# Hybrid attention block on one core: weight differences on VectorE, projections placed between block products, gate products moved behind the scores

## The chip, the core and the metric

The kernel runs on one core of a Trainium2 chip. TensorE (PE, with its weight loads shown as PEld) multiplies matrices into PSUM; VectorE (DVE), ScalarE (ACT) and GpSimd (POOL) do elementwise work; SyncE (SP) issues most of the loads. The metric is the time of one execution on the device in microseconds.

## The reference

One transformer block on 512 tokens of width 1024, in float32. The input is normalised (rmsnorm) and multiplied by one wide matrix `w_in`, whose columns are split into the parts of two branches:

```python
n = rmsnorm(h, g_mix[l])
proj = n @ w_in[l]
(gq, gk, gv, gr, z_gf, z_gb, cq, ckv, kr, z_ma, z_mb) = jnp.split(proj, SPLIT_IDX, axis=-1)
...
merged = jax.nn.sigmoid(z_ma) * y_gla + jax.nn.sigmoid(z_mb) * y_mla
h = h + merged @ w_out[l]
m = rmsnorm(h, g_mlp[l])
h = h + jnp.square(jax.nn.relu(m @ w_ff1[l])) @ w_ff2[l]
```

The first branch is a gated linear attention (GLA) with 4 heads, forward and backward over the tokens. Its decays come from a small gate product, `log_sigmoid(z @ w_gate + b) / 16`, summed along the tokens; query and key are multiplied by exponentials of these sums before their product is formed. Its output is normalised per head and multiplied by `silu(gr)`. The second branch is a latent attention with 8 heads, rotary positions and a softmax (MLA). Each branch is weighted by a sigmoid gate (`z_ma`, `z_mb`). An output product and a squared-ReLU feed-forward part with a residual each follow, and a last rmsnorm.

## The kernel before, in words

**Precision and tiles.** Every float32 operand of a matrix product is split into a rounded high half and a low half (`split`, L92 to L98): ScalarE writes the high half (L93, or L97 with a scale), VectorE subtracts it to get the low half (L94, L98). A product is then three matmuls, high by high, high by low, low by high (`mm3`, L87 to L90). Tiles are 128 partitions by 512 tokens or columns, tile `u2`, or two of these side by side, tile `u4`; both kinds come from pools with a fixed number of buffers (29 and 26). Split weights lie in pools `wh` and `wl` with 4 buffers each, unsplit ones in `wf` with 3. PSUM has two pools, `mm` and `at`, of four banks each.

**Stage 1, first products (up to about 28 us).** The first rows of weights, for gq0, gk0 and two of the MLA gates (zb0, zb1), are multiplied while the input arrives, and the norm of the input is formed.

**Stage 2, three block products (about 28 to 200 us).** The 1024 wide projections gr, za and gv are each formed by `Seven`: both operands are cut into 2 by 2 blocks and seven block products are made in place of eight, in the order `SEVEN = (1, 2, 5, 6, 3, 7, 4)`. The sums and differences of the input blocks are made once (`x_sums`, `more_x_sums`, tiles xy, xz, split to xsy, xsz). The weights come as four blocks of two tiles each (`load`), and four of the seven products use a difference of blocks, made in place by `less` (L571 to L575) on POOL, two instructions of 128x1024 each, so 24 instructions in all. `prepare(m)` makes the difference if one is needed and splits the block; `product(m)` runs the 24 matmuls, for each of two row blocks rb and each of four input tiles p, and then copies or adds the accumulators (L615, L620) and hands finished rows to a sink: `gr_rows` (L628, L629), `za_rows` (L633, L635) or `gv_rows` (L97, L98). Accumulators xs and zs each serve several of the seven products one after the other. The loop (L907 to L926) prepares two steps ahead. The projection zb3 (`zb_gate(3)`) stands behind product 7 of gr, gq1 (`project_qk(1, 0)`) behind product 7 of gv. `gate_parts(0, "mm")` stands behind product 3 of gv.

**Stage 3, four GLA heads (about 200 to 360 us).** For each head h the loop (L931 to L981) emits: `gla_scores` (product bd and its copy bds on ACT, L497; four tiles sc with matmuls L505, L506, L507; a masked overwrite from bds, L511; a split); `gla_turn` of the head before (transposes, tile y, L678); `project_qk(h + 1, 1)` (gk of the next head); `gate_parts(h + 1)`; `gla_out` (48 matmuls, squares L660 and gating L662, then the norm factor on POOL, L663 to L665, and four scalings of the output rows on POOL, L668); for the first two heads `zb_gate(4 + h)` and `project_qk(h + 2, 0)`; `gla_qk` of the next head. `gate_parts` is a chain: gate product L410, Abs, Exp, Ln on ACT (L411, L415, L416), a scan on VectorE (L425), small copies on POOL (L436 to L438), Exp on ACT (L433, L434, L440). `gla_qk` then multiplies query and key by these on VectorE (L454), and POOL makes from them the factors for neighbouring and far chunks (L462, eight instructions per head). For head 2, `rotary_tables` stands ahead of the scores: the positions are loaded by a DMA that POOL issues (L730), VectorE forms the angle (L732 to L743), ACT sine and cosine (L744, L745). For the last head the latent projections ckv and cq come ahead of the scores; `latent` is a generator that yields halfway through its first projection.

**Stages 4 to 6.** MLA attention, the output product and the feed-forward part, from about 360 us to the end.

**What sets the order.** The instructions of an engine run in order. The framework places them, but helpers pin the order of some: `in_program_order(ordered, PE_ONLY)` at L927 pins TensorE to the written order through stage 2, the next line pins POOL from `x_sums` to there, and `goes_behind` (L124) puts a group behind another. In stage 3 TensorE's order is pinned only in these places. Loads stand on SP's queue and wait there for a free buffer.

Of the kernel before, what the change touches and what calls it, by code (L numbers as in the profile page):

```python
# [14 lines left out]
AF = mybir.ActivationFunctionType  # L15
# [3 lines left out]
P = 128  # L19
# [37 lines left out]
def tile_block(ctx: ExitStack, tc: tile.TileContext, t, out: bass.AP):  # L57
# [49 lines left out]
    def traced():  # L107
        return len(nc.cur_bb.bb.instructions)
# [447 lines left out]
    class Seven:  # L556
# [13 lines left out]

        def less(self, dst, x, y):  # L571
            for g in range(2):
                nc.gpsimd.tensor_tensor(  # L573
                    self.blocks[dst][g], self.blocks[x][g], self.blocks[y][g], op=ALU.subtract
                )  # L575

# [17 lines left out]
        def product(self, m):  # L594
            if m == 1:
                self.xs = [ps("at", f"{self.name}x{rb}") for rb in range(2)]
                self.c11, self.c12, self.c22 = ([u2(f"{self.name}{c}") for _ in range(2)] for c in "abc")
            elif m == 2:
                self.ws = [ps("mm", f"{self.name}w{rb}") for rb in range(2)]
            elif m == 5:  # L600
                self.zs = [ps("at", f"{self.name}z{rb}") for rb in range(2)]
            accs = {2: "ws", 5: "zs", 3: "zs"}.get(m, "xs")
            accs = getattr(self, accs)
            begin = m in (1, 2, 5)
            right = self.right.pop(m)
            for rb in range(2):
                acc, tok = accs[rb], slice(rb * P, (rb + 1) * P)
                for p in range(KD // 2):
                    lh, ll = x_left[p][m]
                    wh, wl = right[p // 2]  # L610
                    mm3(acc, lh[:, tok], ll[:, tok], wh[:, p % 2, :], wl[:, p % 2, :],
                        begin and p == 0, p == KD // 2 - 1, not begin)
                if m in (1, 5, 6):
                    c = {1: self.c11, 5: self.c22, 6: self.c12}[m][rb]
                    nc.scalar.activation(c, acc, AF.Copy)  # L615
                elif m == 4:
                    self.sink(2 + rb, 0, acc, u2(f"{self.name}d"))
                else:
                    c = {2: self.c11, 3: self.c12, 7: self.c22}[m][rb]
                    nc.vector.tensor_tensor(c, acc, c, op=ALU.add)  # L620
                    self.sink(rb + (2 if m == 7 else 0), int(m != 2), c, c)
# [23 lines left out]
    def gla_out(h, sc):  # L645

        half, at = h // 2, (h % 2) * GDV
        accs = [ps("at", f"gla{h}o{j}") for j in range(2)]
        c = slice(at, at + GDV)
        for i in range(NT):  # L650
            o = accs[i // 2][:, (i % 2) * GDV : (i % 2 + 1) * GDV]
            tok = slice(i * P, (i + 1) * P)
            for j in range(NT):
                mm3(o, sc[j][:, 0, tok], sc[j][:, 1, tok], v[j, half][:, 0, c], v[j, half][:, 1, c],
                    j == 0, j == NT - 1)
        tot = sm(f"gla{h}ss")
        for i in range(NT):
            o = accs[i // 2][:, (i % 2) * GDV : (i % 2 + 1) * GDV]
            junk = u2(f"gla{h}sq")
            nc.scalar.activation(junk[:, 0:GDV], o, AF.Square, accum_out=tot[:, i : i + 1])  # L660
            g = g1[i, half][:, c]
            nc.vector.tensor_tensor(g, o, g, op=ALU.mult)  # L662
        nc.gpsimd.tensor_scalar(tot, tot, 1.0 / GDV, EPS, op0=ALU.mult, op1=ALU.add)  # L663
        nc.gpsimd.tensor_tensor(tot, tot, mhalf.to_broadcast([P, NT]), op=ALU.pow)
        nc.gpsimd.tensor_tensor(tot, tot, r_x, op=ALU.mult)  # L665
        for i in range(NT):
            g = g1[i, half][:, c]
            nc.gpsimd.tensor_scalar(g, g, tot[:, i : i + 1], None, op0=ALU.mult)  # L668

    def gla_turn(h, early=None):  # L670

# [16 lines left out]
    def latent(col, n, gcol, name):  # L688
        cs, sqs = [], []
        for j in range(n):  # L690
            if j == 0:
                begun = proj_begin(w_in, col, f"{name}0")
                proj_run(begun, xT, None, range(KD // 2))
                yield
                acc = proj_run(begun, xT, None, range(KD // 2, KD))
            else:
                acc = proj_T(col + j * P, f"{name}{j}")
            c = u2(f"{name}c{j}")
            nc.scalar.activation(c, acc, AF.Copy, scale=gvec[:, gcol + j : gcol + j + 1])
            s = u2(f"{name}s{j}")  # L700
            nc.scalar.activation(s, acc, AF.Square)
            if sqs:
                nc.vector.tensor_tensor(s, s, sqs[-1], op=ALU.add)
            cs.append(c)
            sqs.append(s)
        yield
        diag = feature_rstd(sqs[-1], n * P, name, True)
        yield
        rs = spread(diag, name, "mm")
        res = []  # L710
        for j in range(n):
            nc.vector.tensor_tensor(cs[j], cs[j], rs, op=ALU.mult)
            hl = u4(f"{name}hl{j}")
            split(hl[:, 0, :], hl[:, 1, :], cs[j])
            res.append(hl)
        yield res
# [176 lines left out]
    def zb_gate(f):  # L893
        g2.append(gated(proj_T(C_ZB + f * P, f"zb{f}"), f"b{f}")[1])
# [5 lines left out]
    summed = traced()  # L900
    x_sums()
    zb_gate(2)
    steps = [(a, m) for a in range(3) for m in SEVEN]
    ordered = traced()
    for a, m in steps[:2]:
        sevens[a].prepare(m)
    for n, (a, m) in enumerate(steps):  # L907
        if n + 2 < len(steps):
            b, mm = steps[n + 2]
            if a + 1 < 3:  # L910
                for x in {3: (0,), 7: (2, 1), 4: (3,)}.get(m, ()):
                    sevens[a + 1].load(x)
        if m == 7:
            sevens[a].product(m)
            if a == 0:
                zb_gate(3)
            elif a == 2:
                project_qk(1, 0)
        if n + 2 < len(steps):
            sevens[b].prepare(mm)  # L920
            if n == 0:
                more_x_sums()
        if m != 7:
            sevens[a].product(m)
        if a == 2 and m == 3:
            parts = gate_parts(0, "mm")  # L926
    in_program_order(ordered, PE_ONLY)  # L927
    in_program_order(summed, (mybir.EngineType.Pool,))
    near, nxt, far = gla_qk(0, parts)
    scored = None  # L930
    for h in range(GH):  # L931
        last = h == GH - 1
        began = traced()
        if h == GH - 2:
            cos, sin = rotary_tables()
        if last:
            ckv_steps, cq_steps = latent(C_CKV, 2, V_KV, "ckv"), latent(C_CQ, 3, V_Q, "cq")
            next(ckv_steps)
            next(ckv_steps)
            marks = [traced()]  # L940
            next(cq_steps)
            marks.append(traced())
            next(ckv_steps)
            marks.append(traced())
            next(cq_steps)
            goes_behind((marks[1], marks[2]), (marks[0], marks[1]), PE_ONLY)
            goes_behind((marks[2], traced()), (marks[1], marks[2]), PE_ONLY)
            ckv = next(ckv_steps)
            next(cq_steps)
            zb = proj_T(C_ZB + 6 * P, "zb6")  # L950
        projected = traced()
        sc = gla_scores(near, nxt, far)
        scored = traced()
        goes_behind((projected, scored), (began, projected), PE_ONLY)
        if h:
            gla_turn(h - 1, (projected, scored))
        if last:
            g2.append(gated(zb, "b6")[1])
            spreading = traced()
            cq = next(cq_steps)  # L960
            goes_behind((spreading, traced()), (projected, scored), PE_ONLY)
            kbuf = rotary_k()
            zb = proj_begin(w_in, C_ZB + 7 * P, "zb7")
            at = traced()
            proj_run(zb, xT, None, range(3))
            mid = traced()
            ro = rotary_q()
            goes_behind((mid, traced()), (at, mid), PE_ONLY)
            g2.append(gated(proj_run(zb, xT, None, range(3, KD)), "b7")[1])
            for _ in up_units(0):  # L970
                pass
            gla_out(h, sc)
        else:
            project_qk(h + 1, 1)
            parts = gate_parts(h + 1)
            gla_out(h, sc)
            if h < 2:
                zb_gate(4 + h)
            if h < 2:
                project_qk(h + 2, 0)  # L980
            near, nxt, far = gla_qk(h + 1, parts)  # L981
    LAG_B, LAG_C = 3, 6
    units = iter(())
# [367 lines left out]
```

## Time and profile before

| | |
|---|---|
| median of 3 runs | 824.61 us (821.28 to 826.24) |
| the profiled execution | 824.34 us, span 822.6 us |
| granted clock, mean over the span | 0.974 |
| PE / PEld busy | 772.7 / 646.2 us |
| DVE / ACT / POOL busy | 605.0 / 450.7 / 202.6 us |
| POOL on `less` (L573), 24 instructions | 70.6 us |

The span runs from the first to the last instruction of the profiled execution. A row of a group names the line, the engine, the operation and the tiles (output, arrow, inputs), then the total and the mean of one instruction, then the idle time of the engine ahead of it and what ended that. A row of the waits names who waited for whom, the total, how often, and the longest. A row of a stretch gives its length, then busy time and number of instructions of PE, PEld, DVE, ACT and POOL, the granted clock of TensorE, and the DMA share and rate. A row of the timeline gives start, duration and instruction, and in brackets the idle time before it.

### The profile page before, as it was taken

Reading aid. Unit: us, or ns where it says so; the run is one execution under the profiler, and the core shown is the slowest. Engines: PE = TensorE matmul, PEld = TensorE weight load, DVE = VectorE, ACT = ScalarE, POOL = GpSimd, SP = SyncE. Lnnn points to the kernel's source line nnn. Section 1 sums busy time; section 2 is a strip of 40 time slices with the busy share of each in tenths; the row PEclk is TensorE's granted clock in tenths of the full one; section 3 lists DMA queues with packets and bytes.
Section 4 is the critical chain, followed back from the end, with each engine's and each line's share of the span. In section 5 each row is a group of like instructions: output and inputs, shape, how many; then the busy total and the mean of one; then the engine's idle time right before and its main releaser. Section 6 shows DMA issues by size and latency. Waiting matters only on the chain.

```text
span 822.6 us, 10202 instructions
## 1 busy us (share of the span) xinstructions
PE 772.7 (94%) x3744; PEld 646.2 (79%) x3744; DVE 605.0 (74%) x838; ACT 450.7 (55%) x761; POOL 202.6 (25%) x230
## 2 busy tenths in 40 slices
PE   9976999978978889999999999999999999999996
PEld 7755777857867678898888888888888888888885
DVE  7898689997746474779997367795679567956795
ACT  7654455564635373579885246643564356435654
POOL 1884273725437062333112010000000000000014
PEclk9997999998989799999999999999999999999998
DMA  7814313003012103134203363136213611360002
GB/s 251 287 58 131 99 51 103 1 26 104 26 51 78 39 8 51 33 71 135 65 26 129 103 233 101 51 103 197 60 51 103 202 55 51 104 203 26 27 1 102
DMA packets 87042, 73.95 MB, mean 90 GB/s; under 512 B 15088, under 2 KB 66288, under 8 KB 86992
## 3 DMA queue, kind: packets, MB, share of 16 engines
q1 hardware_dynamic: 85904, 70.14, 28.5%
q10 hardware_dynamic: 864, 2.38, 0.8%
q0 software_dynamic: 224, 0.79, 0.3%
q8 instruction: 29, 0.48, 0.2%
q14 instruction: 21, 0.17, 0.1%
HBM read 69.62 MB, written 2.10 MB: 87 GB/s over the span
## 4 chain that ended last, share of the span: by engine, by line
PE 70%; DVE 13%; ACT 6%; POOL 6%; issue 3%; DMA 0%; POOLq 0%; DVEq 0%; ACTq 0%
PE f L89 7%; PE f L90 7%; PE f L88 7%; PE gx L88 4%; PE gx L90 4%; PE gx L89 4%; PE first L312 2%; POOL qk L462 2%; PE wo L89 2%; PE wo L88 2%; PE gz L90 2%; PE gz L89 2%; PE wo L90 2%; PE gz L88 2%; PE tp L870 2%
## 5 line engine op out<-in xcount | busy, mean ns | idle before, releaser
L1290 POOL DMA_DIRECT2D gfin<-in_g_final x1 | 0.7, 661 | 282.7 <-PE f L90 282.7
L1115 DVE TENSOR_TENSOR w<-w,w 128x1024 f32<-128x1024 f32 x32 | 38.7, 1220 | 0.4
L573 POOL TENSOR_TENSOR zaw<-zaw,zaw 128x1024 f32<-128x1024 f32 x8 | 22.2, 2801 | 32.8 <-DVE za10l L94 20.7
L573 POOL TENSOR_TENSOR gvw<-gvw,gvw 128x1024 f32<-128x1024 f32 x8 | 25.0, 3164 | 18.9 <-DVE gv10l L94 14.3
L573 POOL TENSOR_TENSOR grw<-grw,grw 128x1024 f32<-128x1024 f32 x8 | 23.4, 2955 | 3.2 <-DVE gr50l L94 3.0
L888 POOL TENSOR_TENSOR tb<-tb,y 128x512 f32<-128x512 f32 x8 | 11.2, 1402 | 50.3 <-DVE tb L887 36.0
L856 ACT ACTIVATE e<-s,top 128x512 f32<-128x512 f32 x32 | 22.1, 693 | 2.4 <-DVE top L853 2.3
L1062 DVE TENSOR_TENSOR h<-gx,h 128x512 f32<-128x512 f32 x32 | 21.5, 683 | 1.9 <-PE gx L90 1.8
L94 DVE TENSOR_TENSOR pT<-tp,pT 128x512 fp32r<-128x512 f32 x32 | 21.6, 678 | 1.0 <-ACT pT L93 0.7
L853 DVE TENSOR_REDUCE top<-s 128x1 f32<-128x512 f32 x32 | 21.7, 679 | 0.1
L93 ACT ACTIVATE pT<-tp 128x512 fp32r<-128x512 f32 x32 | 19.2, 600 | 3.4 <-PE tp L870 3.4
L870 PE MATMUL tp<-ident,e 128*128 128x128 f32 x128 | 19.3, 273 | 0.1
L88 PE MATMUL av<-pT,v 128*128 128x256 f32 x64 | 19.1, 299 | 0.0
L436 POOL COPY v3f<-rrf 128x4 f32<-128x4 f32 x4 | 0.9, 234 | 72.5 <-DVE rrf L425 72.5
L1168 ACT ACTIVATE fa<-f 128x512 f32<-128x512 f32 x32 | 18.5, 578 | 0.0
L89 PE MATMUL av<-pT,v 128*128 128x256 f32 x64 | 18.4, 287 | 0.0
L90 PE MATMUL av<-pT,v 128*128 128x256 f32 x64 | 18.2, 285 | 0.0
L870 PEld LDWEIGHTS tp<-ident,e 128*128 128x128 f32 x128 | 15.3, 140 | 3.7 <-PE s L90 0.6
L93 ACT ACTIVATE gbh<-y 128x512 fp32r<-128x512 f32 x16 | 10.1, 634 | 14.0 <-DVE y L1185 14.0
L506 PE MATMUL sc<-qk 128*128 128x128 f32 x32 | 8.6, 362 | 9.8 <-POOL qk L462 9.8
L93 ACT ACTIVATE sc<-sc 128x512 fp32r<-128x512 f32 x16 | 9.2, 594 | 15.5 <-DVE sc L511 15.5
L506 PEld LDWEIGHTS sc<-qk 128*128 128x128 f32 x32 | 6.8, 264 | 10.4 <-POOL qk L462 10.4
(1637 smaller groups left out, 2995.3 us busy)
## 6 DMA issues: line engine op xcount, KB each, us to landing
w<-in_w_ff SPq DMA_DIRECT2D x64, 256.0 KB, 3.3
grw<-in_w_in SPq DMA_DIRECT2D x8, 512.0 KB, 9.1
zaw<-in_w_in SPq DMA_DIRECT2D x8, 512.0 KB, 3.9
gvw<-in_w_in SPq DMA_DIRECT2D x8, 512.0 KB, 4.2
x<-in_xt SPq DMA_DIRECT2D x8, 256.0 KB, 5.4
vw<-in_w_first SPq DMA_DIRECT2D x8, 256.0 KB, 5.6
h<-in_x ACTq DMA_DIRECT2D x4, 512.0 KB, 5.2
out<-ms SPq DMA_DIRECT2D x7, 256.0 KB, 2.2
```

Of the source, the lines that this page charges most:

```text
L88: nc.tensor.matmul(acc, lh, rh, start=start, stop=False, skip_group_check=onto)
L89: nc.tensor.matmul(acc, lh, rl, start=False, stop=False, skip_group_check=onto)
L90: nc.tensor.matmul(acc, ll, rh, start=False, stop=stop, skip_group_check=onto)
L93: nc.scalar.activation(hi, src, AF.Copy)
L94: rest.tensor_tensor(lo, src, raw(hi), op=ALU.subtract)
L573: nc.gpsimd.tensor_tensor(self.blocks[dst][g], self.blocks[x][g], self.blocks[y][g], op=ALU.subtract)
L853: nc.vector.tensor_reduce(top, acc, axis=AX.X, op=ALU.max, negate=True)
L856: nc.scalar.activation(e, acc, AF.Exp, bias=top, accum_out=tot)
L870: nc.tensor.transpose(tp[:, k * P : (k + 1) * P], e[:, k * P : (k + 1) * P], ident)
L1062: nc.vector.tensor_tensor(hc, acc, hc, op=ALU.add)
L1115: nc.vector.tensor_tensor(wq[dst][g], wq[x][g], wq[y][g], op=op)
L1168: nc.scalar.activation(a, acc, AF.Relu)
```

## The change

`less` issues its subtractions on VectorE. `product` runs the input tiles in the outer loop and the two row blocks in the inner one, and handles both accumulators after all 24 matmuls. The four scalings at the end of `gla_out` go from POOL to ACT. The projections that stand between block products are listed in a table: zb3 behind product 2 of gr, zb4 behind product 7 of gr, gq1 behind product 7 of za, gk1 behind product 7 of gv, zb5 behind product 4 of gv; in a step with such a projection the product and the projection come ahead of the preparation two steps on. In the heads, `gate_parts(h + 1)` uses pool `mm` and stands directly behind the scores and transposes; for heads 0 and 1 gq of head h + 2 follows, then `gla_out`, then gk of head h + 2; for head 2 the first projection of ckv, whole, and then `gla_out`. `latent` yields behind its first projection rather than halfway. TensorE's written order is now pinned from stage 2 to `gla_out` of head 2. The diff, all of it:

```diff
--- before.py
+++ after.py
@@ -570,7 +570,7 @@
 
         def less(self, dst, x, y):
             for g in range(2):
-                nc.gpsimd.tensor_tensor(
+                nc.vector.tensor_tensor(
                     self.blocks[dst][g], self.blocks[x][g], self.blocks[y][g], op=ALU.subtract
                 )
 
@@ -603,13 +603,14 @@
             accs = getattr(self, accs)
             begin = m in (1, 2, 5)
             right = self.right.pop(m)
-            for rb in range(2):
-                acc, tok = accs[rb], slice(rb * P, (rb + 1) * P)
-                for p in range(KD // 2):
-                    lh, ll = x_left[p][m]
-                    wh, wl = right[p // 2]
-                    mm3(acc, lh[:, tok], ll[:, tok], wh[:, p % 2, :], wl[:, p % 2, :],
+            for p in range(KD // 2):
+                lh, ll = x_left[p][m]
+                wh, wl = right[p // 2]
+                for rb in range(2):
+                    tok = slice(rb * P, (rb + 1) * P)
+                    mm3(accs[rb], lh[:, tok], ll[:, tok], wh[:, p % 2, :], wl[:, p % 2, :],
                         begin and p == 0, p == KD // 2 - 1, not begin)
+            for rb, acc in enumerate(accs):
                 if m in (1, 5, 6):
                     c = {1: self.c11, 5: self.c22, 6: self.c12}[m][rb]
                     nc.scalar.activation(c, acc, AF.Copy)
@@ -665,7 +666,7 @@
         nc.gpsimd.tensor_tensor(tot, tot, r_x, op=ALU.mult)
         for i in range(NT):
             g = g1[i, half][:, c]
-            nc.gpsimd.tensor_scalar(g, g, tot[:, i : i + 1], None, op0=ALU.mult)
+            nc.scalar.activation(g, g, AF.Copy, scale=tot[:, i : i + 1])
 
     def gla_turn(h, early=None):
 
@@ -690,9 +691,8 @@
         for j in range(n):
             if j == 0:
                 begun = proj_begin(w_in, col, f"{name}0")
-                proj_run(begun, xT, None, range(KD // 2))
+                acc = proj_run(begun, xT)
                 yield
-                acc = proj_run(begun, xT, None, range(KD // 2, KD))
             else:
                 acc = proj_T(col + j * P, f"{name}{j}")
             c = u2(f"{name}c{j}")
@@ -900,42 +900,39 @@
     summed = traced()
     x_sums()
     zb_gate(2)
+    fillers = {
+        (0, 2): lambda: zb_gate(3), (0, 7): lambda: zb_gate(4), (1, 7): lambda: project_qk(1, 0),
+        (2, 7): lambda: project_qk(1, 1), (2, 4): lambda: zb_gate(5),
+    }
     steps = [(a, m) for a in range(3) for m in SEVEN]
     ordered = traced()
     for a, m in steps[:2]:
         sevens[a].prepare(m)
     for n, (a, m) in enumerate(steps):
-        if n + 2 < len(steps):
-            b, mm = steps[n + 2]
-            if a + 1 < 3:
-                for x in {3: (0,), 7: (2, 1), 4: (3,)}.get(m, ()):
-                    sevens[a + 1].load(x)
-        if m == 7:
+        ahead = steps[n + 2] if n + 2 < len(steps) else None
+        filled = (a, m) in fillers
+        if a + 1 < 3:
+            for x in {3: (0,), 7: (2, 1), 4: (3,)}.get(m, ()):
+                sevens[a + 1].load(x)
+        if filled:
             sevens[a].product(m)
-            if a == 0:
-                zb_gate(3)
-            elif a == 2:
-                project_qk(1, 0)
-        if n + 2 < len(steps):
-            sevens[b].prepare(mm)
+            fillers[a, m]()
+        if ahead:
+            sevens[ahead[0]].prepare(ahead[1])
             if n == 0:
                 more_x_sums()
-        if m != 7:
+        if not filled:
             sevens[a].product(m)
         if a == 2 and m == 3:
             parts = gate_parts(0, "mm")
-    in_program_order(ordered, PE_ONLY)
     in_program_order(summed, (mybir.EngineType.Pool,))
     near, nxt, far = gla_qk(0, parts)
-    scored = None
     for h in range(GH):
         last = h == GH - 1
-        began = traced()
         if h == GH - 2:
             cos, sin = rotary_tables()
+        began = traced()
         if last:
-            ckv_steps, cq_steps = latent(C_CKV, 2, V_KV, "ckv"), latent(C_CQ, 3, V_Q, "cq")
-            next(ckv_steps)
             next(ckv_steps)
             marks = [traced()]
             next(cq_steps)
@@ -971,13 +968,16 @@
                 pass
             gla_out(h, sc)
         else:
-            project_qk(h + 1, 1)
-            parts = gate_parts(h + 1)
-            gla_out(h, sc)
-            if h < 2:
-                zb_gate(4 + h)
+            parts = gate_parts(h + 1, "mm")
             if h < 2:
                 project_qk(h + 2, 0)
+                gla_out(h, sc)
+                project_qk(h + 2, 1)
+            else:
+                ckv_steps, cq_steps = latent(C_CKV, 2, V_KV, "ckv"), latent(C_CQ, 3, V_Q, "cq")
+                next(ckv_steps)
+                gla_out(h, sc)
+                in_program_order(ordered, PE_ONLY)
             near, nxt, far = gla_qk(h + 1, parts)
     LAG_B, LAG_C = 3, 6
     units = iter(())
```

## The prediction, made before the change was run

> **What bounds the kernel now.** I read the page's busy line and its groups first, then the waits of TensorE, then the busy time by stretches, then the order of instructions around each long wait.
>
> ```profile
> span 822.6 us, 10202 instructions
> PE 772.7 (94%) x3744; PEld 646.2 (79%) x3744; DVE 605.0 (74%) x838; ACT 450.7 (55%) x761; POOL 202.6 (25%) x230
> L1115 DVE TENSOR_TENSOR w<-w,w 128x1024 f32<-128x1024 f32 x32 | 38.7, 1220 | 0.4
> L573 POOL TENSOR_TENSOR zaw<-zaw,zaw 128x1024 f32<-128x1024 f32 x8 | 22.2, 2801 | 32.8 <-DVE za10l L94 20.7
> L573 POOL TENSOR_TENSOR gvw<-gvw,gvw 128x1024 f32<-128x1024 f32 x8 | 25.0, 3164 | 18.9 <-DVE gv10l L94 14.3
> L573 POOL TENSOR_TENSOR grw<-grw,grw 128x1024 f32<-128x1024 f32 x8 | 23.4, 2955 | 3.2 <-DVE gr50l L94 3.0
> ```
>
> TensorE (PE) is busy 94% of the span, so the time can only shrink where it stands still or runs slowly. The change touches the stretch from about 28 to 346 us. TensorE's waits there:
>
> ```profile
> PE sc L506 <- POOL qk L462: 9.8, 3, 4.4
> PE grx L89 <- DVE gr60l L94: 9.8, 1, 9.8
> PE ckvss L255 <- DVE ckvs L703: 3.9, 1, 3.9
> PE sc L505 <- ACT bds L497: 2.8, 1, 2.8
> PE bd L493 <- DVE qkb L454: 1.9, 1, 1.9
> PE zaz L89 <- DVE za30l L94: 1.7, 1, 1.7
> PE gvz L89 <- DVE gv30l L94: 1.7, 1, 1.7
> PE zax L89 <- DVE za61l L94: 1.7, 1, 1.7
> PE gvz L89 <- DVE gv31l L94: 1.7, 1, 1.7
> PE grz L89 <- DVE gr50l L94: 1.6, 1, 1.6
> ```
>
> Two kinds stand here. In the block products (gr, za, gv) it is the low half of a split weight on VectorE (DVE) that is late; in the heads it is the qk factors from GpSimd (POOL). The rows add to 36.6 us; waits below 1 us are left out. The clock adds to that: after the 9.8 us wait a matmul takes 0.63 us that takes 0.39 elsewhere (the gate product below, of the same shape), and the granted clock falls in each of these places.
>
> ```profile
> 68.06 0.80 PE L89 MATMUL grx<-gr60l,xsy 128*128 128x512 f32 x1 [9.79 <-DVE gr60l L94]
> 68.65 0.63 PE L90 MATMUL grx<-gr60h,xsy 128*128 128x512 f32 x1
> 58.00:77.00 19.00, 8.83 (x28) 6.41 (x27) 17.56 (x11) 6.23 (x9) 12.23 (x5) 0.73 0.21 58
> 196.00:209.00 13.00, 9.94 (x44) 8.31 (x43) 7.50 (x13) 2.62 (x5) 6.86 (x8) 0.74 0.29 81
> 229.00:239.00 10.00, 6.12 (x26) 5.45 (x27) 2.90 (x7) 2.42 (x5) 4.40 (x6) 0.66 0.22 62
> 267.00:287.00 20.00, 16.43 (x61) 13.32 (x62) 10.17 (x19) 6.40 (x10) 1.99 (x4) 0.74 0.14 41
> 300.00:320.00 20.00, 16.13 (x68) 13.08 (x68) 11.24 (x18) 8.94 (x19) 13.93 (x16) 0.91 0.27 31
> ```
>
> The columns of a stretch are length, busy time of PE, PEld, DVE, ACT, POOL, then the clock. Length times missing clock is at most 5.1, 3.4, 3.4, 5.2 and 1.8 us; part of that fell on an idle engine, so I count 2.8, 2.8, 2.4, 4.7 and 1.7, together 14.4. What can be won at all is thus near 51 us.
>
> Why the low halves are late: stretches with and without a subtraction on POOL.
>
> ```profile
> 52.60:70.20 17.60, 7.81 (x29) 6.14 (x30) 17.60 (x8) 5.42 (x8) 17.60 (x6) 0.81 0.05 12
> 150.30:169.20 18.90, 16.42 (x70) 12.61 (x68) 17.53 (x9) 8.09 (x10) 18.89 (x7) 1.00 0.00 1
> 70.20:89.60 19.40, 17.71 (x69) 13.35 (x68) 15.53 (x19) 12.96 (x17) 0.03 (x1) 0.91 0.66 206
> L94 DVE TENSOR_TENSOR gr61l<-grw,gr61h 128x1024 fp32r<-128x1024 f32 x1 | 3.4, 3378 | 0.0
> L94 DVE TENSOR_TENSOR gr30l<-grw,gr30h 128x1024 fp32r<-128x1024 f32 x1 | 1.2, 1228 | 0.3 <-ACT gr30h L93 0.3
> L620 DVE TENSOR_TENSOR zaa<-zaw,zaa 128x512 f32<-128x512 f32 x2 | 1.4, 678 | 0.0
> ```
>
> In the first two stretches (12 subtractions and one small POOL instruction) VectorE finishes 17 instructions in 35.1 us, 2.07 us each; in the third 19 in 15.5 us, 0.82 each. The same split takes 3.38 us beside POOL and 1.23 without it. L620, one of whose inputs is a PSUM accumulator, keeps 0.68 us even beside POOL.
>
> **The change part by part.** *Subtractions on VectorE.* 24 instructions leave POOL (22.2 + 25.0 + 23.4 = 70.6 us) and come to VectorE at 1.22 us each by L1115, the same shape: 29.3 us more. What VectorE gets back in the two stretches, which hold half of the 24, is 17 × (2.07 − 0.82) = 21 us; over all 24, by count, up to 42, and no less than 21. So VectorE's load in the stage changes by between +8 and −13 us, and I take −10, since every stretch with back-to-back subtractions looks like these two. A weight is ready after 1.2 + 1.0 + 1.2 us instead of 3 + 1.0 + 3.4.
>
> The Trainium skill, SBUF — State Buffer, section "Who interferes with whom", says that a VectorE instruction with two SBUF inputs and a GpSimd instruction that reads SBUF exclude one another for a whole instruction, and that one with a single SBUF input is not held up. The long gr61l and the short L620 agree. By the rule alone up to the whole 70.6 us could come free, which would end all waits of the block products and give some 4 us less than the sum below, inside the forecast's own range.
>
> *Fillers and the order inside a product.* zb3 moves from behind gr7 to behind gr2, zb4, gk1 and zb5 come into the stage, gq1 goes behind za7. Each costs TensorE 24 matmuls at 16.42/70 = 0.235 us, 5.6 us, wherever it stands: zero in sum, but each covers 5.6 us of VectorE's work. Each also brings a split (1.04 ACT, 1.23 DVE) and an evacuation (0.68) with it. Their weights pass SP's queue earlier, one 512 KB load each; zb4's was issued at 89.7 and first read at 188.8, so its cover is about 99 us. Behind gr7 it has hardly any left if it is issued as late as before; the nearest price is the 3.6 us from issue to use of the positions load below. With p outside rb, a product wants its second half-weight 12 matmuls (2.7 us) in rather than 6, frees the first after 12 rather than 18, and ends both accumulators together, so the first accumulator's evacuation starts 2.7 us later. That matters only where the next product adds to the same bank, 7 then 4; a filler now stands between these in all three blocks.
>
> ```profile
> 89.70 0.37 SPq L222 DMA_DIRECT2D zb4f<-in_w_in  x1
> L93 ACT ACTIVATE zb4h<-zb4f x1: 1042/1042/1042, 188.8 to 188.8; 128x1024 fp32r<-128x1024 f32 x1
> ```
>
> It is issued when zb3's split frees its slot, and that split now comes some 30 us earlier, so I charge nothing. Term a, block gr: waits of 1.6 + 9.8 and 2.8 of clock, 14.2. TensorE reached gr6's second matmul at 68.06 − 9.79 = 58.3; without the 1.6 and with zb3 in front it gets there at 62.3, and at the second half-weight 2.7 later. VectorE ended gr5's splits about where the first stretch begins, 52.6, and from there has the four half-size xsz, less6, gr6, zb3 and gra: 2.7 + 2.4 + 2.5 + 1.2 + 1.4 = 10.2, plus 2.4 for less5: near 65 if all of it comes first, near 62 if gra and zb3 do not. gr3 and gr7 follow as closely. I leave 2 us of waits: **−12.2**. What is late next is the second half-weight of gr6, then gr3. Bounds −7 to −14.2. Term b, za and gv: waits of 4 × 1.7; VectorE has 14 × 1.23 + 8 × 1.22 + 14 × 0.68 = 36.5 us of work per block (splits, subtractions, sums and gates) against 7 × 5.6 = 39 of TensorE, and a filler brings 1.9 against 5.6. I leave 2 us: **−4.8**, bounds −6.8 to +6 (two us on three late weights).
>
> *Gate products behind scores, scaling on ACT.* The chain gate product, Exp, Ln, scan, Exp, qk, POOL's factors decides when a head's scores can go on.
>
> ```profile
> 244.04 0.39 PE L410 MATMUL gatef<-z,gate_f 128*128 128x512 f32 x1
> 262.52 2.80 POOL L668 TENSOR_SCALAR gra<-gra,gla1ss 128x256 f32<-128x256 f32 x2
> 265.30 1.81 POOL L668 TENSOR_SCALAR grd<-grd,gla1ss 128x256 f32<-128x256 f32 x2
> 267.74 0.49 PE L506 MATMUL sc<-qk 128*128 128x128 f32 x2 [4.23 <-POOL qk L462]
> 268.21 0.78 POOL L730 DMA_DIRECT2D pos_i<-in_positions  x1
> 271.80 0.43 DVE L732 CAST ang<-pos_i 128x512 f32<-128x512 int32 x1 [8.18 <-DMA pos_i<-in_positions]
> 278.83 0.57 ACT L497 ACTIVATE bds<-bd 128x512 f32<-128x512 f32 x1
> L660 ACT ACTIVATE gla0sq<-gla0o x4: 366/376/384, 220.1 to 222.8; 128x256 f32<-128x256 f32 x4
> ```
>
> From the gate product of head 2 (244.0) to the end of the factors (268.2, when POOL goes on) it is 24.2 us, 4.6 of it the four scalings that POOL now loses: 19.6. TensorE meanwhile has gq and gk, 2 × 5.6, and gla_out, 48 matmuls of half the width or again 5.6: 17, plus 1 of bd (8 matmuls of a quarter): a wait of 1 to 2 us instead of 4. Four scalings on ACT have no row; the nearest is L660, same shape, 0.37, and above it the 0.68 of L620's 128x512 on VectorE: 1.5 to 2.7 us a head, no gain or loss where ACT is half idle. Term c, head 0: its gates stand where they stood, with four products behind them, but no subtractions slow VectorE; of 1.9, the 9.8 − 4.4 − 4.2 = 1.2 of its factors, and 2.8, **−2.5** (0 to −5.9). Term d, head 1: of 4.4 + 2.4, 1.3 stays: **−5.5** (−2 to −6.8). Term e, head 2: old loss 4.2 + 2.8 + 4.7 = 11.7. POOL finishes some 5 us sooner, but the positions load is queued behind the factors, and from its issue to bds it is 10.6 us, with gk3 no longer there to fill: TensorE's order is now fixed through head 2, sc3 needs bds's bank, and gates, ckv0 and gla_out stand behind it. I leave 1 + 7.5 + 2.7 = 11.2: **−0.5** (+6 to −10). Term f, head 3: cq0 whole instead of half ahead of ckvss, 2.7 more cover, of 3.9 + 1.7, hence **−3** (0 to −5.6). Term g: the last head's scalings fall in a stretch where ACT is full, 1.5 us of which I charge **+0.5** (0 to +2.7).
>
> ```profile
> 360.00:380.00 20.00, 19.87 (x127) 17.34 (x126) 17.60 (x37) 19.35 (x48) 10.30 (x15) 1.00 0.24 69
> ```
>
> The sum is −12.2 − 4.8 − 2.5 − 5.5 − 0.5 − 3 + 0.5 = −28.0. The profiled execution took 824.34 us (span 822.6), 0.3 below the median of 824.61, so the forecast is **796.3 us**.
>
> **The rivals.** *Rotary gets out of the way* (chance 0.17): if the framework puts bds ahead of the sine table on ACT, or issues the positions load before the factors, term e becomes −10: 787. For: bds needs only the bd product, nothing of the sine. Against: in the row above it came last, behind both tables, though bd was multiplied before the factors were ready.
>
> *VectorE paces the stage* (0.18): VectorE is full in the stretch around gr6 (17.60 of 17.60) and now carries 1.2 us of subtraction ahead of each split itself; if every second step of gr and a third of za and gv waits 1 to 1.5 us, and the chain of head 0 stays, terms a to c give −6 instead of −19.5: 810. The Trainium skill, Perfetto Trace Analysis, section "Identifying the Most-Contended Engine", would have the engine with the highest occupancy relieved first; by that rule a move onto a VectorE that is 100% busy from 52.6 to 70.2 is wrong. The trace speaks half against it, since 0.82 of 2.07 us there is work and the rest is being held up.
>
> *Slower: the long splits are not POOL's doing* (0.07). Place: 40 to 180 us. VectorE then carries 29.3 us more on top, of which the slack where POOL is silent (19.4 − 15.5 per stretch, three such) takes 12 at best; the heads save 11: 831 to 843, and 834 because the slack is mostly there. Without it, it decides once less than 29.3 − 11 = 18 us of the 21 to 42 come free. Against it: the pairs 3.38 and 1.23 above.
>
> *The gain is handed back* (0.08): the tiles of head 1 and 2 come early but their buffers do not, since more gates and one more gk are held through the heads; the waits only move: 822.
>
> **How the numbers follow.** The forecast has 0.50, its own range 786 to 806. 787, 796 and 810 hold 0.85 of the chance and are all more than 1% (8 us, about what a measurement of this kernel can tell from no change) below 824.6. Same is the fourth rival, 0.08, slower the third, 0.07. With terms a and c at their good ends beside the first rival, and 810 with a little more, the range is 780 to 814.
>
> **What would show it.** Right: no L94 row above 2 us between 60 and 170 us; L573 on DVE at 1.2; POOL below 125 us busy; the 9.8 us wait gone and gr6 below 2; the three qk waits below 2 each. Wrong: za or gv with new waits above 1 us per product, the rotary wait above 12 us, or ckvss as late as before. It fails as a whole if L94 stays long with POOL silent.

## The result, and the profile after

The changed kernel takes 800.62 us (median of 4 runs, 797.92 to 800.86) against 824.59 before: a ratio of 0.9707, 95% interval 0.967 to 0.9743, 24 us faster. The forecast was 796.3 us with a range of 780 to 814. The profiled execution took 800.71 us, its span is 799.0. First the page's busy line, then the subtractions on VectorE (DVE) from the groups between 40 and 180 us, then TensorE's (PE) waits from 28 to 330 us:

```profile
span 799.0 us, 10180 instructions
...
PE 765.6 (96%) x3744; PEld 643.6 (81%) x3744; DVE 587.1 (73%) x862; ACT 458.4 (57%) x777; POOL 118.0 (15%) x190
```
```profile
L573 DVE TENSOR_TENSOR zaw<-zaw,zaw 128x1024 f32<-128x1024 f32 x8 | 9.8, 1223 | 0.2
L573 DVE TENSOR_TENSOR gvw<-gvw,gvw 128x1024 f32<-128x1024 f32 x8 | 9.8, 1222 | 0.2
L573 DVE TENSOR_TENSOR grw<-grw,grw 128x1024 f32<-128x1024 f32 x6 | 7.3, 1213 | 0.0
```
```profile
PE sc L505 <- ACT bds L497: 10.7, 1, 10.7
PE zb L90 <- DVE zb3l L94: 2.9, 1, 2.9
PE ckvss L255 <- DVE ckvs L703: 2.7, 1, 2.7
PE sc L506 <- POOL qk L462: 2.2, 2, 1.2
PE bd L493 <- DVE qkb L454: 1.6, 1, 1.6
PE y L679 <- DVE sc L94: 1.5, 2, 1.3
...
PE sc L507 <- POOL qk L462: 1.0, 2, 0.8
```

VectorE does 24 instructions more and is busy 18 us less. Every wait of the block products is gone but one, at zb3. In the heads the long waits were for POOL's factors (9.8 us in all before, 3.2 now); now the longest, 10.7 us, is for ScalarE's (ACT) copy bds.

Where the 23.6 us of the span went is read from the starts of the same instruction in both traces. Before:

```profile
100.29 0.39 PE L88 MATMUL zax<-za10h,xT 128*128 128x512 f32 x1
...
174.35 0.39 PE L410 MATMUL gatef<-z,gate_f 128*128 128x512 f32 x1
...
208.75 0.40 PE L410 MATMUL gatef<-z,gate_f 128*128 128x512 f32 x1
...
237.71 0.38 PE L678 MATMUL y<-ident,gra 128*128 128x128 f32 x2
...
286.67 0.40 PE L410 MATMUL gatef<-z,gate_f 128*128 128x512 f32 x1
...
353.32 0.28 PE L88 MATMUL gla3o<-gv,sc 128*128 128x256 f32 x1
```

After:

```profile
91.74 0.39 PE L88 MATMUL zax<-za10h,xT 128*128 128x512 f32 x1
...
162.46 0.39 PE L410 MATMUL gatef<-z,gate_f 128*128 128x512 f32 x1
...
196.21 0.58 PE L410 MATMUL gatef<-z,gate_f 128*128 128x512 f32 x1
...
221.64 0.41 PE L679 MATMUL y<-ident,gra 128*128 128x128 f32 x2 [1.29 <-DVE sc L94]
...
258.04 0.78 PE L410 MATMUL gatef<-z,gate_f 128*128 128x512 f32 x1
...
328.85 0.28 PE L88 MATMUL gla3o<-gv,sc 128*128 128x256 f32 x1
```

A projection that changed its stretch is worth 5.6 us there, as in the prediction; ckv0's 11 matmuls that used to stand ahead of the gates of head 3 are 2.6.

| stretch, term | difference of the marks | work that came or went | change | predicted |
|---|---|---|---|---|
| to the first za product (a) | −8.6 | +5.6 (zb4) | −14.2 | −12.2 |
| to the gates of head 0 (b) | −3.3 | +5.6 (gq1) | −8.9 | −4.8 |
| to the gates of head 1 (c) | −0.7 | 0 | −0.7 | −2.5 |
| to the transposes of head 0 (d) | −3.5 | 0 | −3.5 | −5.5 |
| to the gates of head 3 (e) | −12.6 | −11.2 (zb5, one gk), −2.6 | +1.2 | −0.5 |
| to gla_out of head 3 (f) | +4.2 | +2.6 | +1.6 | −3 |
| to the end (g) | +0.9 | 0 | +0.9 | +0.5 |

The last column adds to −28.0, the one before it to −23.6. Terms a and c vary between traces of the same code by up to 2.8 us each, as shown further down, so their single figures here are rough.

### The profile page after: what moved, and what is told of

Read it like the earlier page. It is cut to its first block, busy times and chain, and to the rows that moved or that the text cites. A ratio compares the mean times of both kernels' runs of the same rounds, so it can differ in the third digit from the quotient of the medians.

```text
span 799.0 us, 10180 instructions
## 1 busy us (share of the span) xinstructions
PE 765.6 (96%) x3744; PEld 643.6 (81%) x3744; DVE 587.1 (73%) x862; ACT 458.4 (57%) x777; POOL 118.0 (15%) x190
## 4 chain that ended last, share of the span: by engine, by line
PE 76%; DVE 7%; ACT 6%; POOL 5%; issue 2%; DMA 2%; SPq 0%; POOLq 0%; DVEq 0%; ACTq 0%
PE f L89 7%; PE f L90 7%; PE f L88 7%; PE gx L88 4%; PE gx L90 4%; PE gx L89 4%; POOL qk L462 3%; PE wo L90 2%; PE wo L88 2%; PE gz L90 2%; PE gz L88 2%; PE gz L89 2%; PE wo L89 2%; PE tp L870 2%; DMA x<-in_xt 1%
## 5 line engine op out<-in xcount | busy, mean ns | idle before, releaser
L870 PEld LDWEIGHTS tp<-ident,e 128*128 128x128 f32 x128 | 15.5, 140 | 3.6 <-PE s L90 0.4
L505 PE MATMUL sc<-qkf 128*128 128x128 f32 x32 | 7.4, 319 | 10.8 <-ACT bds L497 10.7
L888 POOL TENSOR_TENSOR tb<-tb,y 128x512 f32<-128x512 f32 x8 | 11.2, 1404 | 43.9 <-DVE tb L887 30.5
L505 PEld LDWEIGHTS sc<-qkf 128*128 128x128 f32 x32 | 6.7, 226 | 12.5 <-ACT bds L497 11.6
L88 PE MATMUL s<-kbuf,q 96*128 96x512 f32 x32 | 14.0, 438 | 0.7 <-ACT e L856 0.5
L93 ACT ACTIVATE b_10h<-w 128x1024 fp32r<-128x1024 f32 x7 | 7.4, 1059 | 12.1 <-PE gz L90 6.0
L93 ACT ACTIVATE b_20h<-w 128x1024 fp32r<-128x1024 f32 x7 | 7.4, 1059 | 12.1 <-PE gz L90 6.0
```

What stands on the lines that cost most here:

```text
L88: nc.tensor.matmul(acc, lh, rh, start=start, stop=False, skip_group_check=onto)
L93: nc.scalar.activation(hi, src, AF.Copy)
L870: nc.tensor.transpose(tp[:, k * P : (k + 1) * P], e[:, k * P : (k + 1) * P], ident)
```

## The experiments

Each time is the median of the experiment's own runs beside runs of the kernel before on the same chip, with the ratio to these and its 95% interval. The changed kernel stands at 0.9707 by the same measure. Differences between two experiments are taken from these medians; the ratios would give up to 2 us more or less.

**e1, the subtractions alone.** The kernel before with one edit, as in the diff:

```diff
-                nc.gpsimd.tensor_tensor(
+                nc.vector.tensor_tensor(
```

> The kernel before with the 24 weight differences on VectorE and nothing else changed. Theory (VectorE was held up by GpSimd's subtractions): the splits fall back to 1.2 us, the waits of za and gv (6.8 us) go, of the 9.8 us wait and its slow clock about 5 stay because no projection stands ahead of gr5: 15 us less than before, about 809. Rival (the projections between the products and the product order bring the gain, the engine of the subtraction does not matter): within 4 us of before, 820 to 826. Second rival (VectorE has no room for 29 us more): 5 to 15 us slower than before.

803.83 us, 0.9761 (0.9733 to 0.9789): 19.7 us of the 24. VectorE's busy time falls by 14 us although it has 29.3 more to do, and no split is longer than 2 us. The page's busy line and TensorE's waits:

```profile
PE 770.2 (96%) x3744; PEld 646.9 (80%) x3744; DVE 590.6 (73%) x862; ACT 451.3 (56%) x761; POOL 134.1 (17%) x206
```
```profile
PE sc L506 <- POOL qk L462: 9.4, 3, 4.4
...
PE grz L89 <- DVE gr50l L94: 2.0, 1, 2.0
...
PE grx L89 <- DVE gr60l L94: 1.2, 1, 1.2
```

The 9.8 us wait becomes 1.2 with no projection in front of it; za and gv have no wait above 1 us. Both rivals are out. It is 5 us better than my own theory said, which had left 5 us of waiting at gr6.

**e2, all but the subtractions.** The changed kernel with `less` on POOL again:

```diff
-                nc.vector.tensor_tensor(
+                nc.gpsimd.tensor_tensor(
```

> The changed kernel with the 24 weight differences back on GpSimd. Theory: splits beside a subtraction take about 3.4 us again, waits return in gr, za and gv, partly covered by the projections: 10 to 18 us more than the changed kernel, 811 to 819. Rival (projections and order bring the gain): at most 4 us more, 800 to 805.

822.68 us, 0.9999 (0.9986 to 1.0013): nothing at all is left of the gain, 3 to 4 us worse than expected. TensorE's waits:

```profile
PE sc L505 <- ACT bds L497: 10.7, 1, 10.7
PE zb L90 <- DVE zb3l L94: 10.6, 1, 10.6
PE zb L88 <- ACT zb3h L93: 5.8, 1, 5.8
...
PE zaz L89 <- DVE za30l L94: 2.6, 1, 2.6
PE gvz L89 <- DVE gv30l L94: 2.6, 1, 2.6
```

The wait that stood at gr6 now stands at zb3, 16.4 us in two parts. Putting a projection in front of a late product covers nothing if its own weights are split by the engine that is late.

**e3, contention without dependence.** The changed kernel; behind each subtraction on VectorE, POOL subtracts as many elements into a tile that nothing reads:

```diff
+                for j in range(2):
+                    spare = tl([P, NT, P + 1], F32, "rr", 2, "spare")
+                    nc.gpsimd.tensor_tensor(
+                        spare[:, :, 1:], self.blocks[dst][g][:, j, :].rearrange("p (a b) -> p a b", a=NT),
+                        raw(xT[g])[:, j, :].rearrange("p (a b) -> p a b", a=NT), op=ALU.subtract
+                    )
```

> The changed kernel, where behind each of the 24 subtractions on VectorE GpSimd also subtracts as many elements into a tile that nothing reads; the output is the same. Theory (being held up, not the later weight, is the cost): VectorE's splits are long again although no weight waits for GpSimd, 12 to 25 us more than the changed kernel, 813 to 826. Rival (in the kernel before the weights were late only because the subtraction itself took 3 us on GpSimd): within 3 us of the changed kernel, 798 to 804.

827.0 us, 1.004 (1.0025 to 1.0055): 26 us more than the changed kernel, 1 past my range. The longest groups of each engine:

```profile
L573 DVE TENSOR_TENSOR grw<-grw,grw 128x1024 f32<-128x1024 f32 x7 | 13.7, 1959 | 0.0
```
```profile
L578 POOL TENSOR_TENSOR spare<-gvw,xT 128x512 f32<-128x512 f32 x16 | 33.8, 2139 | 17.8 <-DVE gvw L573 17.8
```

VectorE's own subtractions in gr stretch from 1.21 to 1.96 us, and the whole gain is gone although no split or matmul waits for POOL's idle work. So the cost before was VectorE being held up, not the 3 us a subtraction took. Elsewhere the stretching is of another size: the subtractions of za and gv take 1.47 us on average, and many splits beside POOL's work 2.31 instead of 1.22. The idle work is also not quite without consequence: four weight loads on SP's queue wait for POOL to finish reading a buffer, 11.9 us in all, but no wait of TensorE, ScalarE or VectorE in this trace names a load of za or gv. POOL's idle work is longer here (100 us in 48 pieces against 70.6 in 24), which may be why it overshoots.

**e4, the rotary tables behind the scores.** The changed kernel with the call moved:

```diff
-        if h == GH - 2:
-            cos, sin = rotary_tables()
         began = traced()
...
         goes_behind((projected, scored), (began, projected), PE_ONLY)
+        if h == GH - 2:
+            cos, sin = rotary_tables()
```

> The changed kernel with the rotary tables written behind the scores of head 2 instead of ahead of them. Theory (the 10.7 us wait for bds is the positions load and the sine table ahead of bds on ScalarE): the wait falls to about 3 us (bds still stands behind the output scalings of head 1, which wait for GpSimd) and the slow clock goes with it: 8 to 11 us less than the changed kernel, 790 to 793. Rival (bds is late because of the factors on GpSimd): the wait stays above 8 us and the time within 2 us.

794.84 us, 0.9653 (0.9631 to 0.9676): 5 us less than the changed kernel. The direction and the wait are as expected (10.7 falls to 3.5), the time is 2 us short of my range; the wait for ckvss has grown to 3.5 us at the same time. In its trace the stretch of term e is 6.7 us shorter than in the changed kernel.

**e5 and e6, the scalings back on POOL**, for all heads (e5) and for head 2 alone (e6):

```diff
-            nc.scalar.activation(g, g, AF.Copy, scale=tot[:, i : i + 1])
+            nc.gpsimd.tensor_scalar(g, g, tot[:, i : i + 1], None, op0=ALU.mult)
```

> The changed kernel with the output scalings of all heads back on GpSimd. Theory: at head 1 the factors wait 4 us longer for them, at head 2 the positions load is issued 4.6 us later and bds with it, while ScalarE no longer waits for GpSimd ahead of the squares of ckv and the wait for ckvss (2.7 us and a slow clock) goes: 1 to 6 us more than the changed kernel, 802 to 806. Rival (the engine of the scaling does not matter, the order of the gates does): within 1.5 us, 799 to 802.

802.87 us, 0.9754 (0.9739 to 0.9769), with these waits; there is none for ckvss:

```profile
PE sc L505 <- ACT bds L497: 15.5, 1, 15.5
PE sc L506 <- POOL qk L462: 5.7, 3, 3.4
```

> The changed kernel with the output scalings of head 2 alone back on GpSimd. Theory (the late ckvss comes from ScalarE, which waits 3.6 us for the norm factor on GpSimd with the squares of ckv queued behind): the wait for ckvss falls from 2.7 to below 1 us and the slow clock goes, 3 to 5 us less, 796 to 798. Rival (the squares are late for another reason, the factors on GpSimd or the split of zb6): the wait stays above 2 us and the time within 1 us.

795.14 us, 0.9659 (0.9642 to 0.9677), 5 us less than the changed kernel and 1 us better than my range, and the wait for ckvss is not in its list either. So moving the scalings to ACT wins at heads 0 and 1 and loses at head 2. With all of them on POOL (e5) the wait for bds is 15.5 instead of 10.7 and that for the factors 3.5 us longer, and the stretches d and e are 4.7 and 4.6 us longer. At the last head the move costs about 1 us: term g is 469.0 us long in e5's trace, 470.15 in the changed kernel's. The trace of the changed kernel shows why head 2 loses. POOL, ACT and VectorE, head 2's start and then head 3's:

```profile
243.86 0.20 POOL L666 TENSOR_TENSOR gla1ss<-gla1ss,r_x 128x4 f32<-128x4 f32 x1
...
244.00 0.77 POOL L730 DMA_DIRECT2D pos_i<-in_positions  x1
...
244.09 0.91 ACT L669 ACTIVATE gra<-gra,gla1ss 128x256 f32<-128x256 f32 x2 [4.17 <-POOL gla1ss L666]
...
253.81 0.58 ACT L497 ACTIVATE bds<-bd 128x512 f32<-128x512 f32 x1
...
279.81 0.91 ACT L669 ACTIVATE grb<-grb,gla2ss 128x256 f32<-128x256 f32 x2 [3.64 <-POOL gla2ss L666]
...
283.42 0.58 ACT L701 ACTIVATE ckvs<-ckv 128x512 f32<-128x512 f32 x1
...
284.13 0.69 DVE L703 TENSOR_TENSOR ckvs<-ckvs,ckvs 128x512 f32<-128x512 f32 x1
```

ACT stands 3.64 us until POOL, whose factors come first, has the norm factor of head 2, and the squares of ckv wait behind; 283.42 and 284.13 are what TensorE's ckvss waits for. The scaling itself is cheap, 0.45 us each.

**e10, the gates of head 0 one product earlier.** The changed kernel:

```diff
-        if a == 2 and m == 3:
+        if a == 2 and m == 6:
```

> The changed kernel with the gate product of head 0 one product earlier, behind product 6 of gv instead of product 3. Theory (head 0 waits because its chain of decays is longer than the four products behind it): the waits of bd and the first scores (3.5 us together) and the slow clock behind them go, 4 to 6.5 us less, 794 to 797. Rival (VectorE is full in that stretch, so the chain ends no earlier): within 1.5 us, and new waits of the last products of gv.

802.07 us, 0.9741 (0.9724 to 0.9759): no gain, as the rival has it. TensorE's waits:

```profile
PE gk L90 <- DVE gk1l L94: 2.5, 1, 2.5
...
PE bd L493 <- DVE qkb L454: 0.5, 1, 0.5
```

The wait for bd falls from 1.6 to 0.5, so the chain does end earlier, against the rival's words, but a new wait of 2.5 stands at gk1's split. That VectorE's queue pays either way fits both rows.

**e9 and e11, both moves.** e9 is e4 with the scalings of heads 0 to 2 written behind bds of the next head; e11 also holds them there on ACT.

```diff
         nc.scalar.activation(bds, bd, AF.Copy)
+        if h:
+            gla_scale(h - 1)
```

> The changed kernel with the rotary tables behind the scores of head 2, as before, and the output scalings of heads 0 to 2 written behind bds of the next head instead of at the end of the output product. Theory (what is left of the wait for bds, 3.5 us, and the late ckvss are both ScalarE standing at the scalings until GpSimd has the norm factor): the wait for bds falls below 1 us, that for ckvss below 1.5, and 4 to 7 us go beside the rotary move alone (794.8): 788 to 791. Rival (bds and ckvss wait for something else): 793 to 796.

787.54 us, 0.9569 (0.9547 to 0.9592): the wait for ckvss is gone. That for bds is 3.5 as in e4, where I had expected less than 1, because the framework still placed head 1's scalings ahead of bds, waiting for POOL until 244.22 us.

> The kernel with both moves (787.5), and the scalings also held behind bds on ScalarE, where the framework had put those of head 1 ahead of it. Theory (bds's last 3.5 us are these scalings waiting for GpSimd): the wait for bds goes, but the transposes of head 1 need the scaled rows, which GpSimd's norm factor allows 3 us after bd, so 1 to 3 us of the wait move there: 784 to 787. Rival (the whole wait only moves): 787 to 789.

785.18 us, 0.954 (0.9513 to 0.9567), the fastest of all, 15 us below the changed kernel; the intervals of e9 and e11 overlap, so what the pin itself adds is not settled. Its wait for bds is gone, and the transposes of head 1 have taken over a part, as expected (second row; the first, for the factors, was 2.2):

```profile
PE sc L512 <- POOL qk L462: 3.7, 3, 1.9
...
PE y L693 <- DVE sc L94: 2.6, 1, 2.6
```

**e7, e12 and e13, the order in a product and the place of zb3.** e7 has the row blocks outside again, e12 has zb3 back behind product 7 of gr, e13 both.

```diff
-            for p in range(KD // 2):
...
-                for rb in range(2):
+            for rb in range(2):
+                acc, tok = accs[rb], slice(rb * P, (rb + 1) * P)
+                for p in range(KD // 2):
```
```diff
-        (0, 2): lambda: zb_gate(3), (0, 7): lambda: zb_gate(4), (1, 7)
+        (0, 7): lambda: (zb_gate(3), zb_gate(4)), (1, 7)
```

> The changed kernel with the old order inside a block product (row blocks outside, input tiles inside). Theory (a product that wants its second half-weight after 6 matmuls instead of 12 waits for it where VectorE is full, in gr only): 0 to 2 us more than the changed kernel, 800 to 803. Rival (the order inside a product carries a good part of the gain): 4 us or more, 805 and up, with waits in za and gv.

809.9 us, 0.9829 (0.9808 to 0.985): 9 us more than the changed kernel, against my theory. Its waits, and the split of zb3 on ACT, which in the changed kernel starts at 48.14:

```profile
PE zb L90 <- DVE zb3l L94: 4.7, 1, 4.7
PE zb L88 <- ACT zb3h L93: 2.7, 1, 2.7
```
```profile
52.28 1.04 ACT L93 ACTIVATE zb3h<-zb3f 128x1024 fp32r<-128x1024 f32 x1
```

> The changed kernel with zb3 back behind product 7 of gr, ahead of zb4. Theory (VectorE's queue, not the place of zb3, sets the first wait): the 2.9 us wait moves from zb3 to gr5 and gr6 and keeps its size within 1.5 us, 799 to 802.5. Rival (zb3 in front gives VectorE 5.6 us it needs, as the prediction has it): 4 to 6 us more and the slow clock of gr6 back, 804 to 809.

800.87 us, 0.9719 (0.9698 to 0.9739), the same as the changed kernel: zb3's place is worth nothing, the wait only moves, to gr6 and gr3:

```profile
PE grx L89 <- DVE gr60l L94: 1.6, 1, 1.6
...
PE grz L89 <- DVE gr30l L94: 1.2, 1, 1.2
```

> The changed kernel with both the old order inside a block product and zb3 back behind product 7 of gr. Theory (the old order frees half-weights later, and it is the split of zb3, a fifth user of four weight buffers while VectorE is full, that pays for it): the 7.4 us wait at zb3 and its slow clock go, 5 to 7 us less than with the old order alone (809.9): 803 to 805. Rival (the old order costs as much without zb3 there): 808 to 811.

805.53 us, 0.9787 (0.9766 to 0.9808): 4.4 us back of the 9.3, just outside my 803 to 805. So the order inside a product is worth about 5 us with zb3 behind product 7 and 9 with it behind product 2. That it is the four weight buffers is argued from e7's late split of zb3, not shown: no run has a fifth buffer.

## Why the prediction was right, and where not

**Right: the cause.** That VectorE was held up by POOL and that 29.3 us more work would leave it with less busy time is shown from both sides: e1 has 19.7 of the 24 us with that edit alone, e2 has none without it, e3 takes it all away with POOL work that no split and no matmul waits for. The Trainium skill, SBUF — State Buffer, section "Who interferes with whom", says that a VectorE instruction with two SBUF inputs contends with a GpSimd one that reads SBUF; e3 agrees: 1.96 us in gr and 1.47 in za and gv in place of 1.21 to 1.22. VectorE's load fell by 14 us in e1; I had taken 10, with a bound of 13.

**Right: the rivals fail.** "VectorE paces the stage" needed waits of 1 to 1.5 us in za and gv, and none above 1 us appeared; "Slower: the long splits are not POOL's doing" falls with e1; "the gain is handed back" falls with the time itself. The rule of the Trainium skill, Perfetto Trace Analysis, section "Identifying the Most-Contended Engine", that the engine with the highest occupancy be relieved first, speaks against e1; the run does not bear it out, since occupancy there counted time in which VectorE was held up.

**Mis-sized: term b,** −8.9 in place of −4.8. I left 2 us of waits; za and gv have none. The waits of this stretch before were 7.0 us in all, and all are gone. The other 1.9 lie mostly in the matmuls' own busy time, 67.00 us for 290 of them before and 70.72 for 314 after, 0.231 and 0.225 us each, which I had counted as fixed.

**Not settled: the sizes of terms a and c.** The traces of the changed kernel and of e4, e5, e6, e9, e10 and e11 have the same code up to the first za product and the same waits there, and reach it between 91.6 and 94.3 us, with different clocks (last section). Term a is thus −14.2 in the trace shown and −11.6 at the other end. The stretch of term c, the same in all of these but e10, takes 30.9 to 33.8 us: −3.5 to −0.6. My −12.2 and −2.5 lie inside both. The kernel before has one trace only.

**Wrong reason in term a.** I put zb3 in front of gr5 as 5.6 us of cover. e12 shows that it covers nothing, and e1 that the wait shrinks to 1.2 us without it: zb3's own weights need the same VectorE. What I left as 2 us of waits came as the 2.9 at zb3.

**Wrong: the order inside a product costs or gains nothing.** I counted a later evacuation and no gain. e7 and e13 show 5 to 9 us.

**Term c, its reason not borne out.** I had put the chain of head 0 down to subtractions that slow VectorE. With them on VectorE, e1 still waits 1.8 us for bd, against 1.9 before and 1.6 in the changed kernel. e10 points to VectorE's queue of splits and sums instead, without showing it.

**Term d, right in kind,** −3.5 for −5.5: the factors' wait fell from 4.4 to 1.0, but the transposes now wait 1.3 us.

**Term e, near as a whole, the wait mis-sized:** +1.2 for −0.5. The rotary wait that I expected (7.5 of fixed wait) came as 10.7. From the issue of the positions load at 244.00 to bds at 253.81 it is 9.8 us, less than the 10.6 before, so ACT's scalings and the split ahead of bds, which lie inside this time, did not lengthen it. My 7.5 left some 3 us of the 10.6 under other work, and there was none: TensorE stood from 243.8 on, before the load was issued. The rival "rotary gets out of the way" did not happen in the change; e4 makes it happen and is worth 5 us. What is left of the wait there, 3.5 us, is ACT standing at the scalings, and goes in e11; e9 and e11 are worth 13 and 15 us.

**Wrong: term f,** +1.6 for −3. I gave cq0's longer cover 2.7 us and asked of the scalings only what they cost ACT, not what they wait for. e6 shows that this wait, 3.64 us of ACT for POOL's norm factor, is the whole of it: in its trace the stretch takes 64.6 us instead of 70.8, which would make the term −4.6.

**Luck in the total.** 796.3 is nearer to 800.6 than the terms are to theirs: b came 4.1 us better than forecast, f 4.6 worse, d 2.0 and e 1.7 worse.

## What to carry to other kernels

Before an engine's long instructions are taken as its load, compare the same form with and without a neighbour at work: 3.38 against 1.23 us said that the move would free more than it cost. An instruction moved to an engine that runs in order brings its wait with it; ask what stands behind it there, as at head 2. A filler in front of a late product did not help where its own weights were made by the late engine. One trace of a kernel is not enough to size a stretch to 2 us: the clock after the same wait differed between executions.

## What the runs showed of the hardware

The clock does not follow the length of a wait alone, and not the code alone. In the changed kernel zb3's wait of 2.9 us left the granted clock at 1.00 (first row). Six other traces, e4, e5, e6, e9, e10 and e11, have the same code up to there and the same wait of 2.9 us; their clock from 45 to 60 us is 1.00 in e10, 0.89 in e5, e6, e9 and e11, and 0.77 in e4 (second row):

```profile
45.00:60.00 15.00, 12.10 (x53) 9.67 (x52) 14.91 (x21) 10.39 (x17) 2.45 (x2) 1.00 0.39 115
45.00:60.00 15.00, 12.14 (x42) 9.49 (x41) 14.57 (x20) 10.20 (x17) 2.29 (x2) 0.77 0.39 115
```

It is the same at head 0, where the code is the same too. In the changed kernel waits of 1.6, 1.2 and 0.8 us between small matmuls stand in a stretch with a clock of 0.90; in e11 the waits are 1.3, 1.2 and 1.1 us, and the clock stays at 1.00:

```profile
162.46:196.21 33.75, 30.22 (x132) 24.79 (x130) 26.31 (x40) 21.52 (x30) 12.55 (x25) 0.90 0.35 94
164.68:195.62 30.94, 27.41 (x132) 22.43 (x130) 26.09 (x39) 21.17 (x30) 12.29 (x25) 1.00 0.38 102
```

In the changed kernel's trace, 13 us around these waits have a clock of 0.74 (first row below), 21 us around the longest wait, 10.7 us at head 2, have 0.67 (second row), and 13 us behind the 2.7 us wait at ckvss have 0.74 (third row):

```profile
184.00:197.00 13.00, 9.47 (x40) 7.81 (x39) 8.40 (x12) 3.96 (x6) 7.77 (x8) 0.74 0.41 108
240.00:261.00 21.00, 10.34 (x48) 8.43 (x47) 12.31 (x23) 10.75 (x18) 4.52 (x9) 0.67 0.15 38
279.00:292.00 13.00, 10.29 (x36) 8.25 (x36) 4.90 (x10) 6.20 (x11) 2.36 (x5) 0.74 0.22 26
```

The Trainium skill, TensorE: Matmul & The Clock Gate, section "What's actually happening", has the clock set by activity in a window of about 3.4 us that runs on by itself, whenever the work starts. Different clocks after the same wait agree with that; no row here shows the window itself.
